# Attention scores issued as pinned pairs of matmuls, and the order of ScalarE's and VectorE's last instructions

## The chip, the cores and the metric

One Trainium2 chip, one of its cores. The metric is the device time of one execution in microseconds. The engines are called by the profile's names: PE is TensorE (matmuls), PEld its weight loads, DVE is VectorE, ACT is ScalarE, POOL is GpSimd, SP is SyncE, which here only starts DMAs.

## What is computed

A trunk of two layers over 256 tokens of width 1024, in float32. Each layer is: half a SwiGLU feed-forward (hidden width 2816), three attentions side by side with a gate each, another half feed-forward, and a gated addition of a second input `p`. At the end there is one more RMS norm.

```
for i in range(2):
    h = h + 0.5 * swiglu(rms_norm(h, g0), ffn1_wi, ffn1_wo)
    n = rms_norm(h, g1); split n @ w_in into the q, k, v, gates of A, B and C
    ya = differential attention (4 heads x 2 score maps, all earlier keys)
    yb = NSA attention (8 heads: compressed keys, selected blocks, window)
    yc = sliding window attention with sinks (8 heads, window 128)
    h = h + (sig(ga) * (ya @ wb0) + sig(gb) * (yb @ wb1) + sig(gc) * (yc @ wb2)) @ w_out
    h = h + 0.5 * swiglu(rms_norm(h, g2), ffn2_wi, ffn2_wo)
    h = h + sig(rms_norm(h, g3) @ w_ple_gate) * (p[i] @ w_ple)
return rms_norm(h, final_norm)
```

All score heads have width 64: `s = q k^T / 8 + bias`, then a masked softmax.

## The kernel before

**Products.** The tokens are two tiles `t` of 128. Every float32 operand `x` is split into a rounded part `hi` and a rest `lo`, both of a reduced type, and a product is three matmuls, `hi hi + hi lo + lo hi` (`mul3`, lines 265 to 268). Weights come in pieces of 128 x 1024 by a DMA on SyncE's queue (line 375). ScalarE makes `hi` of a piece and VectorE `lo` (`split`, lines 256 to 263). `product` (line 402) runs over the contraction's blocks `k` for both token tiles, the second some steps behind the first, and accumulates in one PSUM bank of 512 columns per tile. When a tile is done, a function `done` reads the bank with ScalarE and VectorE.

**Attentions beside the products.** Three generators, `attend_a`, `attend_c` and `attend_b`, each handle units of four score rows: `first` makes the scores and the softmax of a unit, `second` turns the probabilities and multiplies them with the values of the unit before. After each step of a product `flow.tick()` lets the running generator go on by a piece, so that attention work and products alternate in the program's text. `flow.join` finishes a generator where its result is needed. Each layer calls `scores` fourteen times: four units of A, four of C, six of B.

**scores (line 958).** A call takes two PSUM banks, `ps[0]` and `ps[1]`, from the tag `s`, which has two buffers in all, so the next call needs the same two banks again. For two blocks of heads `m`, for the three products `(x, y)` of hi and lo, and for `par` 0 and 1, it issues one matmul: the contraction is 64 rows deep, and `par` chooses the upper or lower 64 rows of the array. Half `par` writes to `ps[par]`. So twelve matmuls are written per call, with the two halves alternating in the text. They have 128 columns where only one key tile is visible (token tile 0 of A and C), and 256 elsewhere. `softmax` (line 972) reads the four rows one after the other on VectorE (line 978), `ps[0]` first, then `ps[1]`, and ScalarE takes the exponential (line 980).

**What sets the order.** The kernel is written as one program, and a planner decides the order on each engine before it runs. The planner simulates the engines with estimates of its own. Whenever an engine is free, it gives it, among the instructions whose inputs and buffers are ready, the one with the lowest turn; the turn is the place in the text. Two things change that. `tc.high_priority(offset=n)` moves what is written inside it n turns ahead. `tc.keep_in_program_order(ins)` puts `ins` behind the instruction written just before it on the same engine; it orders the issue and waits for no completion, and others may still come in between. On the chip each engine then runs its instructions in the planned order and waits on semaphores. In the kernel before, the score matmuls have neither: each of the twelve takes its own turn.

**The last product.** In the second layer the gate product of the last addition (`ple`, line 1519) runs its second half of columns with `last_product` (line 390): first token tile 0 with 512 columns, then token tile 1 in two quarters of 256, here called third and last quarter. Each ends in `gate.done` (line 1534): tanh on ScalarE (line 1537), the gate product with `pp` on VectorE (line 1538), then `residual_last.done` (line 509): the residual added into `h` on VectorE (line 512), the sum of squares on ScalarE (line 514), for the third quarter also the product of `h` with the final norm's weight into `hg` (`finish`, line 537) and two small sums of statistics (lines 517, 518). The last quarter closes the statistics (line 521), GpSimd takes the power -1/2 (line 522), and `finished` (line 539) scales the rows and sends them out on the queues of ScalarE and SyncE.

Of the kernel before, what the change touches and what calls it, by code (L numbers as in the profile page):

```python
# [13 lines left out]
AF = mybir.ActivationFunctionType  # L14
ALU = mybir.AluOpType
AX = mybir.AxisListType

D, SEQ, DEPTH = 1024, 256, 2
PLE, DFF = 256, 2816
EPS = 1e-6  # L20
# [197 lines left out]
def trunk(ctx: ExitStack, tc: tile.TileContext, a: dict, out: bass.AP, index: list):  # L218
    nc = tc.nc
# [30 lines left out]
    def stage(name="stage"):  # L250
        return base.tile([128, 512], F32, tag="stage", bufs=4, name=name)
# [169 lines left out]
    class Norm:  # L421
# [44 lines left out]
        def square(self, t, c):  # L466
            sq = stage("sq")
            nc.scalar.activation(sq, h[:, t, 512 * c:512 * c + 512], AF.Square, accum_out=self.stat[t][:, c:c + 1])

        def finish(self, t):  # L470
            st = self.stat[t]
            nc.vector.tensor_scalar(st[:, 2:3], st[:, 0:1], 1.0 / D, EPS, op0=ALU.mult, op1=ALU.add)
            nc.vector.scalar_tensor_tensor(st[:, 2:3], st[:, 1:2], 1.0 / D, st[:, 2:3], op0=ALU.mult, op1=ALU.add)
            nc.gpsimd.tensor_tensor(st[:, 3:4], st[:, 2:3], mhalf[:, 0:1], op=ALU.pow)
            nc.vector.tensor_scalar(st[:, 4:5], st[:, 3:4], 0.5, None, op0=ALU.mult)
            nc.vector.tensor_scalar(st[:, 5:6], st[:, 3:4], 0.125, None, op0=ALU.mult)
# [13 lines left out]
    def residual(norm, c, scale, final=False):  # L490

        s = slice(512 * c, 512 * c + 512)

        def done(t, ps):
            nc.vector.scalar_tensor_tensor(h[:, t, s], ps, scale(t), h[:, t, s], op0=ALU.mult, op1=ALU.add)
            if final:
                finish(t, 0, 512)
            elif c == 0 and norm.row % 2:
                norm.turn_late(t)
            else:  # L500
                norm.turn(t, c)
            norm.square(t, c)
            if c == 1:
                norm.finish(t)
        return done

    def residual_last(norm, scale):

        def done(t, x, s):
            o = slice(512 + s.start, 512 + s.stop)  # L510
            st = norm.stat[t]
            nc.vector.scalar_tensor_tensor(h[:, t, o], x, scale(t), h[:, t, o], op0=ALU.mult, op1=ALU.add)
            sq = stage("sq")[:, :s.stop - s.start]
            nc.scalar.activation(sq, h[:, t, o], AF.Square, accum_out=st[:, 6:7] if s.start else st[:, 1:2])
            if s.stop < 512:
                finish(t, 512, 768)
                nc.vector.tensor_scalar(st[:, 2:3], st[:, 0:1], 1.0 / D, EPS, op0=ALU.mult, op1=ALU.add)
                nc.vector.scalar_tensor_tensor(st[:, 2:3], st[:, 1:2], 1.0 / D, st[:, 2:3], op0=ALU.mult, op1=ALU.add)
                return
            if s.start:  # L520
                nc.vector.scalar_tensor_tensor(st[:, 2:3], st[:, 6:7], 1.0 / D, st[:, 2:3], op0=ALU.mult, op1=ALU.add)
                nc.gpsimd.tensor_tensor(st[:, 3:4], st[:, 2:3], mhalf[:, 0:1], op=ALU.pow)
            else:
                norm.finish(t)
            finished(t, s.start, norm.r(t))
        return done

    last = []

    def finish(t, start, stop):  # L530

        if not last:
            last.append(base.tile([128, SUB], F32, tag="raw", bufs=RAWS, name="gfin"))
            nc.sync.dma_start(last[0], rows(a["gfin"], [[1, D]]))
            last.append(base.tile([128, NT, D], F32, tag="blk", bufs=6, name="hg"))
        gfin, hg = last
        nc.vector.tensor_tensor(hg[:, t, start:stop], h[:, t, start:stop], gfin[:, start:stop], op=ALU.mult)

    def finished(t, extra, r):

        gfin, hg = last
        y = [stage("out") for _ in range(2)]
        nc.scalar.activation(y[0], hg[:, t, :512], AF.Copy, scale=r)
        o = slice(512 + extra, 1024)
        nc.vector.scalar_tensor_tensor(y[1][:, extra:], h[:, t, o], r, gfin[:, o], op0=ALU.mult, op1=ALU.mult)
        if extra:
            nc.vector.tensor_scalar(y[1][:, :extra], hg[:, t, 512:512 + extra], r, None, op0=ALU.mult)
        for k, queue in enumerate((nc.scalar, nc.sync)):
            queue.dma_start(out[t * 128:(t + 1) * 128, 512 * k:512 * k + 512], y[k])
# [366 lines left out]
    def attention(i, norm, after):  # L916
# [41 lines left out]
        def scores(name, q, qb, t, key):  # L958

            ps = [psum.tile([128, 2, 256], F32, tag="s", bufs=2, name=name) for _ in range(2)]  # L960
            for m in range(2):
                for x, y in ((0, 0), (0, 1), (1, 0)):
                    for par in range(2):
                        r = slice(64 * par, 64 * par + 64)
                        kk = key(y, r, m)
                        o = ps[par][:, m, :math.prod(kk.shape[1:])]
                        if len(kk.shape) == 3:
                            o = o.rearrange("p (s n) -> p s n", s=kk.shape[1])
                        nc.tensor.matmul(o, q[r, x, qb[m], t * 128:(t + 1) * 128], kk, start=x + y == 0, stop=x == 1)  # L969
            return ps  # L970

        def softmax(p, ps, bias, sink=None):
# [57 lines left out]
        def attend_a():  # L1030
            bnd = band(0)

            def first(u):
                m, t = u
                nk = 128 * (t + 1)
                s = scores("s", qk[m], [0, 1], t, lambda x, r, k: qk[m][r, x, 2 + k, :nk])
                yield
                p = pool.tile([128, 4, 256], F32, tag="p", bufs=3, name="p")
                st = None
                for st in softmax([p[:, j, :nk] for j in range(4)], [s[j // 2][:, j % 2, :nk] for j in range(4)],  # L1040
                                  [back(bnd[:, 2 * m + j % 2], nk) for j in range(4)]):
                    yield
                nc.vector.reciprocal(st[:, 8:12], st[:, 4:8])
                nc.vector.tensor_scalar(st[:, 10:12], st[:, 10:12], nlam[:, i:i + 1], None, op0=ALU.mult)
                for x in range(2):
                    nc.vector.tensor_scalar(p[:, 2 + x, :nk], p[:, 2 + x, :nk], st[:, 10 + x:11 + x], None, op0=ALU.mult)
                    nc.vector.scalar_tensor_tensor(p[:, x, :nk], p[:, x, :nk], st[:, 8 + x:9 + x], p[:, 2 + x, :nk],
                                                   op0=ALU.mult, op1=ALU.add)
                yield
                return p  # L1050
# [221 lines left out]
        def attend_b():  # L1272
            bnd, y_ps = {}, {}

            def first(u):
# [3 lines left out]
                if t == 0:  # L1279
                    p = pool.tile([128, 4, 2, 128], F32, tag="p", bufs=3, name="p")  # L1280
                    s = scores("s", qB[0], [2 * g, 2 * g + 1], 0, lambda x, r, m: kB[0][r, x, g:g + 3:2, :128])
                    rows = [(j, k) for j in range(4) for k in range(2)]
                    pr = [p[:, j, k] for j, k in rows]
                    sr = [s[j // 2].rearrange("p m (k n) -> p m k n", k=2)[:, j % 2, k] for j, k in rows]
                    br = [back(bnd[g][:, j], 128) for j, k in rows]
                else:
                    p = pool.tile([128, 4, 256], F32, tag="p", bufs=3, name="p")
                    s = scores("s", qB[0], [2 * g, 2 * g + 1], 1, lambda x, r, m: kB[0][r, x, 2 * ss[0] + g, :])
                    pr = [p[:, j] for j in range(4)]
                    sr = [s[j // 2][:, j % 2] for j in range(4)]  # L1290
                    br = [back(bnd[g][:, j], 256) for j in range(4)]
# [265 lines left out]
    h = base.tile([128, NT, D], F32, name="h")  # L1557
# [17 lines left out]
    def rows(src, steps):  # L1575
        return bass.AP(tensor=src.tensor, offset=src.offset, ap=[[0, 128]] + steps)
# [141 lines left out]
```

## Time and profile before

| | us |
|---|---|
| median of 3 runs | 1306.7 |
| lowest and highest | 1305.04, 1307.22 |
| the profiled execution | 1305.41 |
| its span | 1303.6 |
| mean granted clock of TensorE in it | 0.998 |

The span reaches from the first to the last instruction of the profiled execution. In a row of the page's groups or of the timeline stand the line of the kernel, the engine, the operation, the tiles written and read, and the shapes (`64*128 64x256` is a stationary operand of 64 rows and 128 columns and a moving one of 64 rows and 256 columns). Starts are microseconds from the beginning of the span. Matmuls overlap in their pipeline, so the time one of them costs is the distance to the start of the next, not its own duration; the chain of waits counts in that way. In the chain in order of time, a row is start, time added to the chain, engine, tile written, line, and xN for N equal instructions in a row.

### The profile page before, as it was taken

The page shows a single profiled execution, that of the slowest core. Times are in us where ns is not written, and L with a number is a line of the kernel's source. Part 1 is how long each engine was busy: PE and PEld are TensorE (multiplying, and loading weights), DVE is VectorE, ACT ScalarE, POOL GpSimd, SP SyncE. Part 2 cuts the span into 40 slices and gives each one's busy share as a digit, 9 for nine tenths or more (in the row PEclk, how much of TensorE's full clock was granted, in tenths as well). Part 3 has the DMA queues.
Part 4 walks back from the last instruction along what each step waited for, and adds up shares of the span by engine and source line. Part 5 has one row for each costly group of instructions (what it writes and reads, how often), then busy time and mean ns, then how long its engine had stood idle before and what let it go on. Part 6 is the DMA issues. An engine that isn't in the chain of part 4 may idle for free.

```text
span 1303.6 us, 17964 instructions
## 1 busy us (share of the span) xinstructions
PE 1293.1 (99%) x6250; PEld 1067.2 (82%) x6250; DVE 1092.4 (84%) x1754; ACT 923.6 (71%) x1468; POOL 28.7 (2%) x46
## 2 busy tenths in 40 slices
PE   9999999999999999999999999999999999999997
PEld 7888888887888888888888888888888888888886
DVE  7878977768978799997799999677687888999975
ACT  7677667658858577876667876666696775877664
POOL 0000000000000000000000000000000000000000
PEclk9999999999999999999999999999999999999999
DMA  8778787455743567687666787865556435677772
GB/s 318 227 230 267 203 262 221 125 181 173 227 151 108 181 191 239 213 239 213 210 196 228 208 248 234 249 175 163 176 173 199 162 129 182 205 211 230 230 231 85
DMA packets 137180, 263.76 MB, mean 202 GB/s; under 512 B 71670, under 2 KB 77174, under 8 KB 137088
## 3 DMA queue, kind: packets, MB, share of 16 engines
q1 hardware_dynamic: 134128, 252.57, 62.7%
q0 software_dynamic: 2528, 9.47, 2.2%
q8 instruction: 49, 0.80, 0.3%
q10 hardware_dynamic: 432, 0.56, 0.1%
q14 instruction: 43, 0.35, 0.1%
HBM read 245.75 MB, written 1.08 MB: 189 GB/s over the span
## 4 chain that ended last, share of the span: by engine, by line
PE 98%; DMA 0%; issue 0%; ACT 0%; SPq 0%; DVE 0%; POOLq 0%; POOL 0%; DVEq 0%; ACTq 0%
PE ff L267 8%; PE ff L266 8%; PE ff L268 8%; PE fo L267 5%; PE fo L266 5%; PE fo L268 5%; PE p L266 4%; PE p L268 4%; PE p L267 4%; PE gate L266 4%; PE gate L268 3%; PE gate L267 3%; PE s L969 3%; PE A L267 2%; PE br L266 2%; PE A L266 2%
## 5 line engine op out<-in xcount | busy, mean ns | idle before, releaser
L254 DVE TENSOR_TENSOR wl<-raw,wh 128x1024 fp32r<-128x1024 f32 (+1 forms) x426 | 510.1, 1211 | 96.2 <-ACT wh L259 94.5
L259 ACT ACTIVATE wh<-raw 128x1024 fp32r<-128x1024 f32 (+1 forms) x426 | 441.7, 1047 | 152.1 <-DMA raw<-in_wst 66.1
L267 PE MATMUL ff<-wl,nT 128*128 128x512 f32 x464 | 180.9, 390 | 0.0
L268 PE MATMUL ff<-wh,nT 128*128 128x512 f32 x464 | 180.3, 390 | 0.0
L266 PE MATMUL ff<-wh,nT 128*128 128x512 f32 x464 | 171.7, 390 | 0.0
L268 PE MATMUL fo<-wh,gT 128*128 128x512 f32 x304 | 117.1, 389 | 0.0
L267 PE MATMUL fo<-wl,gT 128*128 128x512 f32 x304 | 115.7, 389 | 0.0
L266 PE MATMUL fo<-wh,gT 128*128 128x512 f32 x304 | 114.2, 390 | 0.0
L267 PEld LDWEIGHTS ff<-wl,nT 128*128 128x128 f32 x464 | 87.1, 188 | 18.2 <-DVE wl L254 0.2
L268 PEld LDWEIGHTS ff<-wh,nT 128*128 128x128 f32 x464 | 87.1, 188 | 18.0
L266 PEld LDWEIGHTS ff<-wh,nT 128*128 128x128 f32 x464 | 87.1, 188 | 18.0
L268 PE MATMUL gate<-wh,nT 128*128 128x512 f32 x192 | 76.6, 399 | 0.0
L266 PE MATMUL gate<-wh,nT 128*128 128x512 f32 x192 | 76.4, 399 | 0.0
L267 PE MATMUL gate<-wl,nT 128*128 128x512 f32 x192 | 75.8, 395 | 0.0
L268 PEld LDWEIGHTS fo<-wh,gT 128*128 128x128 f32 x304 | 57.1, 188 | 11.8
L266 PEld LDWEIGHTS fo<-wh,gT 128*128 128x128 f32 x304 | 57.1, 188 | 11.7
L267 PEld LDWEIGHTS fo<-wl,gT 128*128 128x128 f32 x304 | 57.1, 188 | 11.7
L980 ACT ACTIVATE p<-p,st 128x128 f32<-128x128 f32 (+1 forms) x128 | 56.7, 449 | 5.3 <-DVE st L978 5.0
L568 ACT ACTIVATE whole<-flip 128x1024 uint16<-128x1024 uint16 x32 | 43.0, 1365 | 20.4 <-DMA flip<-cut 20.3
L562 ACT ACTIVATE cut<-gated 128x1024 uint16<-128x1024 uint16 (+1 forms) x48 | 46.3, 974 | 9.9 <-DVE gated L608 9.9
L254 DVE TENSOR_TENSOR wl<-x,wh 128x1024 fp32r<-128x1024 f32 x42 | 50.5, 1219 | 2.5 <-ACT wh L259 2.5
L259 ACT ACTIVATE wh<-x 128x1024 fp32r<-128x1024 f32 x42 | 43.7, 1048 | 7.0 <-DVE x L254 5.8
(395 smaller groups left out, 2780.5 us busy)
## 6 DMA issues: line engine op xcount, KB each, us to landing
raw<-in_wst SPq DMA_DIRECT2D x424, 512.0 KB, 4.4
y<-in_wst POOLq DMA_DIRECT2D x6, 1024.0 KB, 6.8
band<-table SPq DMA_DIRECT2D x10, 512.0 KB, 5.2
xy<-in_wst POOLq DMA_DIRECT2D x4, 512.0 KB, 4.1
raw<-in_wbv SPq DMA_DIRECT2D x4, 420.0 KB, 3.2
xt<-in_xt SPq DMA_DIRECT2D x4, 256.0 KB, 5.5
raw<-in_wst SPq DMA_DIRECT2D x4, 256.0 KB, 5.0
h<-in_x SPq DMA_DIRECT2D x2, 512.0 KB, 8.0
```

The lines of the kernel that those rows point to most:

```text
L254: nc.vector.tensor_tensor(o, x, y, op=ALU.subtract)
L259: nc.scalar.activation(hi, src, AF.Copy)
L266: nc.tensor.matmul(ps, xh, wh, start=start, stop=False, **kw)
L267: nc.tensor.matmul(ps, xh, wl, start=False, stop=False, **kw)
L268: nc.tensor.matmul(ps, xl, wh, start=False, stop=stop, **kw)
L562: nc.scalar.activation(cut.rearrange("p (w n) -> p w n", w=2), halves(src)[:, :128 * m].rearrange("p n w -> p w n"), AF.Copy)
L568: tc.keep_in_program_order(nc.vector.tensor_copy(to, of) if late else nc.scalar.activation(to, of, AF.Copy))
L969: nc.tensor.matmul(o, q[r, x, qb[m], t * 128:(t + 1) * 128], kk, start=x + y == 0, stop=x == 1)
L980: nc.scalar.activation(p[j], p[j], AF.Exp, bias=st[:, j:j + 1], scale=-1.0, accum_out=st[:, n + j:n + j + 1])
```

## The change

`scores` puts its matmuls two to twelve 300 turns ahead and behind one another; the first keeps its own turn and is tied to nothing. In the tail, the third quarter's square, `hg` product and small sums are written into a function `rest`, which is kept in `put_off` and called only when the last quarter's tanh, gate product and residual have been written. That residual and the `hg` product are tied to their place in the order of VectorE. The last quarter's square carries the factor 1/D itself (a scale of D to the power -1/2 before squaring), so that the last small operation is a plain sum.

```
+            add = nc.vector.scalar_tensor_tensor(h[:, t, o], x, scale(t), h[:, t, o], op0=ALU.mult, op1=ALU.add)
+            if put_off:
+                tc.keep_in_program_order(add)
+                put_off.pop()()
             sq = stage("sq")[:, :s.stop - s.start]
-            nc.scalar.activation(sq, h[:, t, o], AF.Square, accum_out=st[:, 6:7] if s.start else st[:, 1:2])
+
+            def square():
+                nc.scalar.activation(sq, h[:, t, o], AF.Square, scale=D ** -0.5 if s.start else 1.0,
+                                     accum_out=st[:, 6:7] if s.start else st[:, 1:2])
+
             if s.stop < 512:
-                finish(t, 512, 768)
-                nc.vector.tensor_scalar(st[:, 2:3], st[:, 0:1], 1.0 / D, EPS, op0=ALU.mult, op1=ALU.add)
-                nc.vector.scalar_tensor_tensor(st[:, 2:3], st[:, 1:2], 1.0 / D, st[:, 2:3], op0=ALU.mult, op1=ALU.add)
+                def rest():
+                    square()
+                    finish(t, 512, 768)
+                    nc.vector.tensor_scalar(st[:, 2:3], st[:, 0:1], 1.0 / D, EPS, op0=ALU.mult, op1=ALU.add)
+                    nc.vector.scalar_tensor_tensor(st[:, 2:3], st[:, 1:2], 1.0 / D, st[:, 2:3], op0=ALU.mult, op1=ALU.add)
+                put_off.append(rest)
                 return
+            square()
             if s.start:
-                nc.vector.scalar_tensor_tensor(st[:, 2:3], st[:, 6:7], 1.0 / D, st[:, 2:3], op0=ALU.mult, op1=ALU.add)
+                nc.vector.tensor_tensor(st[:, 2:3], st[:, 6:7], st[:, 2:3], op=ALU.add)
                 nc.gpsimd.tensor_tensor(st[:, 3:4], st[:, 2:3], mhalf[:, 0:1], op=ALU.pow)
...
-    last = []
+    last, put_off = [], []
...
-        nc.vector.tensor_tensor(hg[:, t, start:stop], h[:, t, start:stop], gfin[:, start:stop], op=ALU.mult)
+        x = nc.vector.tensor_tensor(hg[:, t, start:stop], h[:, t, start:stop], gfin[:, start:stop], op=ALU.mult)
+        if start:
+            tc.keep_in_program_order(x)
...
-                        nc.tensor.matmul(o, q[r, x, qb[m], t * 128:(t + 1) * 128], kk, start=x + y == 0, stop=x == 1)
+                        with tc.high_priority(offset=0 if (m, x, y, par) == (0, 0, 0, 0) else 300):
+                            ins = nc.tensor.matmul(o, q[r, x, qb[m], t * 128:(t + 1) * 128], kk, start=x + y == 0, stop=x == 1)
+                        if (m, x, y, par) != (0, 0, 0, 0):
+                            tc.keep_in_program_order(ins)
```

More of the change, by code (lines that the diff above doesn't have):

```diff
@@ L511, in done @@
             st = norm.stat[t]
-            nc.vector.scalar_tensor_tensor(h[:, t, o], x, scale(t), h[:, t, o], op0=ALU.mult, op1=ALU.add)
+            add = nc.vector.scalar_tensor_tensor(h[:, t, o], x, scale(t), h[:, t, o], op0=ALU.mult, op1=ALU.add)
+            if put_off:
+                tc.keep_in_program_order(add)
+                put_off.pop()()
             sq = stage("sq")[:, :s.stop - s.start]
-            nc.scalar.activation(sq, h[:, t, o], AF.Square, accum_out=st[:, 6:7] if s.start else st[:, 1:2])
+            def square():
+                nc.scalar.activation(sq, h[:, t, o], AF.Square, scale=D ** -0.5 if s.start else 1.0,
+                                     accum_out=st[:, 6:7] if s.start else st[:, 1:2])
             if s.stop < 512:
-                finish(t, 512, 768)
-                nc.vector.tensor_scalar(st[:, 2:3], st[:, 0:1], 1.0 / D, EPS, op0=ALU.mult, op1=ALU.add)
-                nc.vector.scalar_tensor_tensor(st[:, 2:3], st[:, 1:2], 1.0 / D, st[:, 2:3], op0=ALU.mult, op1=ALU.add)
+                def rest():
[4 more added lines that the diff above has]
+                put_off.append(rest)
                 return
+            square()
             if s.start:
-                nc.vector.scalar_tensor_tensor(st[:, 2:3], st[:, 6:7], 1.0 / D, st[:, 2:3], op0=ALU.mult, op1=ALU.add)
+                nc.vector.tensor_tensor(st[:, 2:3], st[:, 6:7], st[:, 2:3], op=ALU.add)
                 nc.gpsimd.tensor_tensor(st[:, 3:4], st[:, 2:3], mhalf[:, 0:1], op=ALU.pow)
```

## The prediction

> **What bounds the kernel now.** I read the page first, for the engine that sets the end.
>
> ```profile
> span 1303.6 us, 17964 instructions
> PE 1293.1 (99%) x6250; PEld 1067.2 (82%) x6250; DVE 1092.4 (84%) x1754; ACT 923.6 (71%) x1468; POOL 28.7 (2%) x46
> ...
> PE 98%; DMA 0%; issue 0%; ACT 0%; SPq 0%; DVE 0%; POOLq 0%; POOL 0%; DVEq 0%; ACTq 0%
> ```
>
> TensorE is busy for 99% of the span, and the chain that ended last is 98% TensorE. So a nanosecond taken out of TensorE's stream is a nanosecond off the span, as long as no other engine becomes late by it. A busy TensorE can still waste time in how its matmuls follow each other, so the second view is the chain in order of time. There each row is a run of equal instructions with what it added to the chain. These are the score runs (L969) of the first layer, without three more undivided calls of 0.91, 0.91 and 0.92 us.
>
> ```profile
> 211.20 0.37 PE s L969 x3
> 211.56 0.43 PE A L267
> 211.99 0.23 PE A L268
> ...
> 213.15 0.26 PE s L969 x2
> ...
> 214.76 0.26 PE s L969 x2
> ...
> 220.69 0.26 PE s L969 x2
> ...
> 221.85 0.36 PE s L969 x3
> ...
> 226.23 0.91 PE s L969 x12
> 227.14 0.32 PE Ck L268
> 227.46 0.12 PE Ck L266
> ...
> 233.12 0.59 PE s L969 x7
> ...
> 234.09 0.48 PE s L969 x5
> ...
> 261.78 0.82 PE s L969 x12
> ...
> 297.98 1.10 PE s L969 x12
> ...
> 303.33 0.54 PE s L969 x3
> ...
> 304.31 0.55 PE s L969 x3
> ...
> 305.52 0.55 PE s L969 x3
> ...
> 306.49 0.55 PE s L969 x3
> ...
> 316.61 0.31 PE s L969
> ...
> 321.41 0.78 PE s L969 x9
> ...
> 325.42 0.31 PE s L969 x2
> ...
> 330.67 0.91 PE s L969 x6
> ...
> 331.84 0.90 PE s L969 x6
> ...
> 336.68 1.25 PE s L969 x12
> ...
> 386.99 0.55 PE s L969 x6
> ...
> 387.98 0.55 PE s L969 x6
> ...
> 401.36 0.67 PE s L969 x7
> ...
> 404.29 0.54 PE s L969 x5
> ```
>
> A call of `scores` issues twelve matmuls of 64 rows each: for each of two heads `m`, three products, each on both halves `par` of the array's rows. Three things are to be seen. **Order inside a run:** at 226.23 twelve matmuls of 256 columns take 0.91 us; at 330.67 six of the same size take 0.91 us too. Twelve at the price of six is what comes out when neighbours sit on different row halves and run together; the six at 330.67, then six more for 0.90, are one half after the other and run singly. At 336.68 the order is mixed (1.25). **Undivided and paired** a call costs 0.91 us at 256 columns, and 0.82 at 128 columns (261.78). **Each run has a border price:** the first full-height matmul behind a run takes 0.32 instead of 0.12 (227.14 against 227.46), or 0.43 instead of 0.23 (211.56 against 211.99), so 0.20 us for every run, however short.
>
> **The score part, step by step.** Nine of a layer's fourteen calls are divided or out of order. By their rows they cost 0.37+0.26+0.26+0.26+0.36 = 1.51 (five runs), 0.59+0.48 = 1.07 (two), 1.10 (one), 0.54+3x0.55 = 2.19 (four), 0.31+0.78+0.31 = 1.40 (three), 0.91+0.90 = 1.81 (two), 1.25 (one), 0.55+0.55 = 1.10 (two), 0.67+0.54 = 1.21 (two): 12.64 us. Undivided and paired, the first three (128 columns: first token tile of the A and C attentions) would cost 3x0.82 and the other six 6x0.91, 7.92 together: 4.72 less. They make 22 runs where 9 would do: 13 borders of 0.20, 2.60. So at most 7.32 us per layer; the second layer has the same code and the same shapes, so 14.6 for both. The other five calls are already undivided and paired; I cost the edit at nothing there.
>
> What the change does to the order: matmuls two to twelve each stand behind the one before in TensorE's order, and 300 places ahead of their turn. So nothing with a later turn, and little with an earlier one, gets in between once each is ready. That repairs divisions that came from other work having its turn (211.20, 233.12, 316.61, 386.99, 401.36) and the order inside the run. It can't repair a second PSUM bank that is not free yet: the two halves write two banks, and the bank of half 1 comes free later, because the softmax reads half 0 first. The calls at 303.33 and 330.67 finish half 0 before half 1 begins, which is how the plan would look if bank 1 were late. With the pin the first matmul goes alone and eleven follow when bank 1 is free. A single one costs 0.31 (316.61) plus a border of 0.20, about 0.5. The trace has no pinned call, so its price is bounded from both sides: nothing, or 0.5 for each of a layer's fourteen calls, 7.0, which leaves 0.3 of the 7.32. I take 0.5 for the two calls just named and half of it for the two whose order is mixed (297.98 and 336.68): 1.5. That is 7.32 - 1.5 = 5.8 per layer, **11.6 us** for both layers.
>
> Nothing else is issued: the same 336 matmuls, no DMA, nothing on the queues of SyncE or GpSimd. Work that is passed over is moved by less than 1 us at a time; it sits on TensorE too, and its readers are covered as long as the other engines keep their slack (third rival).
>
> **The tail, step by step.** The timeline of the last microseconds:
>
> ```profile
> 1294.85 0.28 PE L268 MATMUL pg<-wh,nT 128*128 128x256 f32 x1
> ...
> 1295.51 0.42 ACT L514 ACTIVATE sq<-h 128x256 f32<-128x256 f32 x1 [0.95 <-DVE h L512]
> ...
> 1295.92 0.46 ACT L1537 ACTIVATE th<-pg,stats 128x256 f32<-128x256 f32 x1
> 1297.39 0.42 ACT L514 ACTIVATE sq<-h 128x256 f32<-128x256 f32 x1 [1.01 <-DVE h L512]
> ```
>
> The last matmul ends at 1294.85 + 0.28 = 1295.13, but the last quarter's tanh begins at 1295.92, behind the third quarter's square, for which ScalarE sat idle. Put ahead of it, the tanh begins up to 0.79 us earlier, and gate product, residual and square follow it. The third quarter's square (1295.92 - 1295.51 = 0.41) then falls into the 1.01 us in which ScalarE waits for the last residual, so it is covered; without that cover it would cost its 0.41. On VectorE the `hg` product and two small sums now come behind the last residual, beside the last square. The product is of the same size as the square (0.42), the sums are small; I put 0.1 for them being late for the statistics. Folding 1/D into the square only replaces one small operation by another. Bounds: -0.1 to +0.8; I take **0.7**, since in the trace the tanh's input is complete before the square's (0.95 us of waiting ended at 1295.51 only), so nothing has to hold the tanh back.
>
> **Sum.** 11.6 + 0.7 = 12.3 us. The profiled execution took 1305.41 us, its span being 1303.6; that gives 1293.1. The shown runs have a median of 1306.7 (1305.04 to 1307.22), 1.3 above it, which gives 1294.4. I forecast **1294**. By the bounds of the two parts the gain is 0.3x2 - 0.1 = 0.5 to 14.6 + 0.8 = 15.4.
>
> **Rivals.**
>
> (1) *The plan breaks most calls into one and eleven*, since bank 1 is late nearly always: the change then does not do what it says. Gain 0.6 + 0.7 = 1.3, so 1305.4. For it: the calls at 303.33 and 330.67. Against: calls such as 226.23 and 261.78 alternate halves from their first matmul without a pin, so both banks were free.
>
> (2) *Slower: TensorE stops in order.* The planner works from its own estimate of VectorE. If a pinned run is issued before the softmax has really left bank 1, TensorE stands still, since it can't pass the waiting matmul; behind it stand all products, and VectorE, ScalarE and the weight buffers wait for those. The price is the reading of half 1's two heads:
>
> ```profile
> L978 DVE CUSTOM_DVE_ANT_0 p<-s,band x96: 280/354/425, 222.4 to 1049.1; 128x128 f32<-128x128 f32 x48, 128x256 f32<-128x256 f32 x48
> ...
>   PEld s L969: 0.7, 2
> ```
>
> Two median reduces are 2 x 0.354 = 0.71 us. It decides from 12.3 / 0.71 = 18 of the 28 calls; in all of them it is 19.9, a loss of 7.6 and 1314.3. Against it: over the whole kernel the score matmuls waited for this reduce twice, 0.7 us in all, as the second row counts.
>
> (3) *Half is given back.* TensorE arrives sooner at the merge of the third attention, and the chain of softmax, turning and gathering is not shortened. The stretches of the attention's second half:
>
> ```profile
> 320.00:380.00 60.00, 60.00 (x338) 50.54 (x337) 50.19 (x117) 40.97 (x88) 0.00 (x0) 1.00 0.64 209
> 380.00:425.00 45.00, 45.00 (x241) 36.33 (x240) 40.54 (x100) 37.66 (x83) 0.00 (x0) 1.00 0.36 116
> ```
>
> The columns are stretch, its length, then busy time of TensorE, weight loads, VectorE and ScalarE. VectorE has 40.54 of 45 us. What I expect to save in a layer's six calls from 316 on is 0.89 + 0.60 + 0.09 + 0.39 + 0.50 = 2.5 (the fifth is already whole). If that comes back as waiting at the merge, 5.0 of the 12.3 are gone: gain 7.3, 1299.4. Against: the saving inside this last stretch is 0.9, and 40.54 of 44.1 is 92%, still short of full. The Trainium skill ("TensorEngine Tiling (Array Packing)", Performance Considerations, PSUM Bottleneck) warns in this sense: packing row tiles makes TensorE faster but not the emptying of PSUM, which may then be the limit. By that rule the time would be that of this rival; the rows so far speak for it only in the last stretch.
>
> **How the numbers follow.** Forecast 0.64 (1289.5 to 1297.5); half given back 0.15; one and eleven 0.11; slower 0.10. The first two hold 0.79, so the range goes from 1289.5 (a gain of 15.4, counted from the lower of the shown runs) to 1300.5. A measurement here can tell about 0.2%, 2.6 us, from no change. Faster: 0.64 + 0.15 + a third of the one-and-eleven case, 0.82; the rest of that case, 0.08, is no change; slower 0.10. The forecast's own gain reaches from 9 to 15.4.
>
> **What would show it.** In the chain after, L969 should fall from 34 us (two layers of 12.64 and the five whole calls' 4.47) to about 25-27, in 28 to 36 rows instead of 54, nearly all of them x12 (0.91, or 0.82 at 128 columns) or x1 followed by x11; rows with x6 of 0.9 should be gone. Rows `x1` in most calls mean rival 1. Idle time of TensorE before L969 released by `st` L978 of several us means rival 2; idle time before `br` or `wo`, released by VectorE's `yB` or `mT`, means rival 3. In the tail, the last tanh should begin within 0.1 us of the last matmul's end, with the third quarter's square behind it; if the square is still ahead, the 0.7 is wrong. A fall of the score rows with an unchanged time would make the whole reading wrong, that TensorE's stream is the time.

## The result and the profile after

| | kernel before | kernel after |
|---|---|---|
| median, us | 1306.59 (4 runs) | 1298.62 (4 runs) |
| lowest and highest | 1305.04, 1307.22 | 1298.43, 1299.48 |
| profiled execution | 1305.41 | 1298.72 |
| its span | 1303.6 | 1296.9 |
| clock of TensorE | 0.998 | 0.998 |

The ratio is 0.9942, with a 95% interval from 0.9925 to 0.9959: 8.0 us by the medians, 6.7 us by the two profiled executions. Timed a second time (below, with another set of the kernel before) the changed kernel had the same median, 1298.62, against 1305.32: 6.7 us. So the gain is 6.7 to 8.0 us where 12.3 were forecast.

The page of the changed kernel: span, busy time of the engines, and the chain that ended last by engine.

```profile
span 1296.9 us, 17954 instructions
PE 1284.1 (99%) x6250; PEld 1062.0 (82%) x6250; DVE 1091.2 (84%) x1754; ACT 922.5 (71%) x1468; POOL 27.6 (2%) x46
...
PE 92%; ACT 3%; DVE 2%; issue 1%; DMA 1%; SPq 0%; POOLq 0%; POOL 0%; DVEq 0%; ACTq 0%
```

TensorE is still busy for 99%, but its share of the chain has gone from 98% to 92%. What is new there is ScalarE 3% and VectorE 2%: at some places TensorE now waits for them. These shares are not waiting time: where TensorE waited, the chain goes back along the engine that it waited for, often for many instructions. The busy row hides this, since 1% of 1297 us is 13 us.

**The score runs.** The chain of the changed kernel in order of time; the columns are start, time added, engine, tile and line (the scores are now line 983), number of instructions. The chain leaves out matmuls that run beside their pair, so a run of eleven can show as x9 or x10.

```profile
226.50 0.82 PE s L983 x12
...
290.74 0.31 PE s L983
291.05 0.43 PE br L266
291.47 0.23 PE br L267
291.71 0.91 PE s L983 x9
...
296.39 0.81 PE s L983 x11
```

No call is in more than two runs, and every twelve or eleven but one has the paired price: 0.90 to 0.91 us, 0.81 to 0.82 at 128 columns. The one, at 968 us, took 1.29 because its second matmul came 0.42 us behind its first. But nine of the 28 calls begin with a single matmul, six in the first layer and three in the second. The one at 290.74 shows the price: 0.31 for itself and 0.43 instead of 0.23 for the first `br` product behind it. Counted by the distances between the starts of TensorE's matmuls, the runs fell from 54 to 37 and their sum from 34.2 to 27.7 us: 6.5, and 17 borders of 0.20, together 9.9 us.

**The waits.** In the stretch in which the compression runs (`cmp`, in each layer 64 matmuls that use up eight pieces of `w1`) beside the end of a gate product, both kernels are shown by their waits (engine and line, what it waited for; us, times, longest), first the changed kernel, then the kernel before:

```profile
PEld gate L267 <- DVE wl L254: 1.3, 1, 1.3
PE gate L267 <- DVE wl L254: 1.0, 1, 1.0
PEld gate L266 <- ACT wh L259: 1.0, 1, 1.0
PE gate L266 <- ACT wh L259: 0.7, 1, 0.7
```

```profile
ACT wh L259 <- PE br L268: 1.4, 1, 1.4
ACT wh L259 <- DMA raw<-in_wst: 0.9, 1, 0.9
...
```

Before, no wait of TensorE for a weight piece stands in the list, and ScalarE waited for TensorE to free a weight buffer; the pieces were ahead. After, TensorE waits for the rounded part `wh` of a piece from ScalarE and for the rest `wl` from VectorE. The windows of these stretches (start and end, length, then busy us with instruction counts of TensorE, weight loads, VectorE, ScalarE, GpSimd, then clock, DMA share, GB/s), changed kernel first:

```profile
318.00:336.00 18.00, 16.25 (x121) 13.80 (x120) 17.44 (x50) 17.88 (x57) 0.00 (x0) 1.00 0.51 163
...
953.00:975.00 22.00, 21.11 (x148) 17.37 (x147) 21.83 (x64) 21.34 (x59) 0.00 (x0) 1.00 0.59 192
```

```profile
318.00:338.00 20.00, 20.00 (x139) 16.98 (x138) 19.47 (x56) 17.34 (x45) 0.00 (x0) 1.00 0.67 223
```

VectorE is busy for 97% here after (17.44 of 18) and was for 97% before (19.47 of 20); ScalarE went from 87% to 99%. So VectorE had no slack in this stretch before the change either. In the second layer's copy of it VectorE has 21.83 of 22 us after. Which work filled them is in the groups of 318 to 336 us, changed kernel first, then the kernel before (line, engine, operation, tiles, shapes, count, busy us and mean ns, idle time before):

```profile
L254 DVE TENSOR_TENSOR wl<-raw,wh 128x1024 fp32r<-128x1024 f32 x7 | 8.4, 1218 | 0.1
L259 ACT ACTIVATE wh<-raw 128x1024 fp32r<-128x1024 f32 x6 | 6.3, 1050 | 0.0
L996 ACT ACTIVATE p<-p,st 128x128 f32<-128x128 f32 x16 | 6.2, 390 | 0.0
...
L1322 DVE TENSOR_SCALAR p<-p,st 128x128 f32<-128x128 f32 x8 | 1.8, 278 | 0.0
```

```profile
L254 DVE TENSOR_TENSOR wl<-raw,wh 128x1024 fp32r<-128x1024 f32 x8 | 9.6, 1216 | 0.8 <-ACT wh L259 0.8
L259 ACT ACTIVATE wh<-raw 128x1024 fp32r<-128x1024 f32 x8 | 8.4, 1052 | 2.2 <-PE br L268 1.4 <-DMA raw<-in_wst 0.9
...
L980 ACT ACTIVATE p<-p,st 128x128 f32<-128x128 f32 x9 | 3.5, 388 | 0.0
```

In the same 18 us ScalarE now makes six pieces instead of eight and VectorE seven instead of eight; sixteen exponentials stand where nine stood, and B's scaling (line 1322, line 1306 before) is there eight times, where its first one came at 339.8 before. In this layer B's first softmax was pulled ahead of weight pieces. Whether that is why the pieces are late is asked below; the second layer differs.

**The account.** By TensorE's starts, in us:

| | score runs and borders | waits | sum | measured |
|---|---|---|---|---|
| first attention part (first `A` product to last `wo`) | -4.4 | 0.86 + 1.21 | -2.3 | -2.07 |
| second attention part | -5.5 | 0.46 + 0.66 + 0.28 + 0.63 | -3.5 | -3.39 |
| tail, last matmul's end to the end of the span | | | | -0.69 |
| all else | | | | -0.5 |

The measured column sums to the span's 6.7. The waits are those at the compression, in both layers, but for the 0.63 at 1055 (`mt`, the transposes at the merge, for `pT` from VectorE). About 4.1 of the 9.9 us came back as waiting, 3.5 of them for weight pieces. The 0.46 does not come every time: it follows a wait of ScalarE for a DMA (`w2raw`, at 941 us) of 1.28 us here, and in the changed kernel's second profile (`e9_changed_again`), with 0.57 us for that DMA, it is absent.

**The tail** of the changed kernel, from the timeline (start, duration, engine, line, operation):

```profile
1288.84 0.28 PE L268 MATMUL pg<-wh,nT 128*128 128x256 f32 x1
...
1289.16 0.47 ACT L1553 ACTIVATE th<-pg,stats 128x256 f32<-128x256 f32 x1 [0.61 <-PE pg L268]
1289.53 0.41 ACT L519 ACTIVATE sq<-h 128x256 f32<-128x256 f32 x1
...
1290.65 0.42 ACT L519 ACTIVATE sq<-h 128x256 f32<-128x256 f32 x1 [0.61 <-DVE h L512]
```

The tanh begins at 1289.16, 0.04 after the last matmul's end (1288.84 + 0.28 = 1289.12), and the third quarter's square lies in ScalarE's wait for the last residual.

### The profile page after: what moved, and what is told of

Its sections match the earlier page's. It is cut to its first block, busy times and chain, and to the rows that moved or that the text cites. A ratio compares the mean times of both kernels' runs of the same rounds, so it can differ in the third digit from the quotient of the medians.

```text
span 1296.9 us, 17954 instructions
## 1 busy us (share of the span) xinstructions
PE 1284.1 (99%) x6250; PEld 1062.0 (82%) x6250; DVE 1091.2 (84%) x1754; ACT 922.5 (71%) x1468; POOL 27.6 (2%) x46
## 4 chain that ended last, share of the span: by engine, by line
PE 92%; ACT 3%; DVE 2%; issue 1%; DMA 1%; SPq 0%; POOLq 0%; POOL 0%; DVEq 0%; ACTq 0%
PE ff L267 8%; PE ff L266 8%; PE ff L268 8%; PE fo L268 5%; PE fo L266 5%; PE fo L267 5%; PE p L266 4%; PE p L267 4%; PE p L268 4%; PE gate L266 3%; PE gate L267 3%; PE gate L268 3%; PE A L267 2%; PE A L268 2%; PE A L266 2%; PE s L983 1%
```

## The experiments

The diffs are against the changed kernel. Each time is compared with the kernel before, timed beside it on the same chip; the chips of different experiments differ. "Score sum" and "runs" are counted as above (before: 34.2 us in 54 runs; after: 27.7 in 37). Two accounts of the lost 4 us stand against each other in the expectations. The theory, T: in the stretch of the compression VectorE and ScalarE are full, so TensorE runs into late weight pieces there, whoever saved its time ahead of it. The rival, R: it is the order; the pins let B's scores, and so B's softmax, come early, and it stands ahead of the weight pieces.

### Scores alone, tail alone

`e1_scores_only` has the new score loop and the old tail, `e2_tail_only` the reverse:

```
-                        with tc.high_priority(offset=0 if (m, x, y, par) == (0, 0, 0, 0) else 300):
-                            ins = nc.tensor.matmul(o, q[r, x, qb[m], t * 128:(t + 1) * 128], kk, start=x + y == 0, stop=x == 1)
-                        if (m, x, y, par) != (0, 0, 0, 0):
-                            tc.keep_in_program_order(ins)
+                        nc.tensor.matmul(o, q[r, x, qb[m], t * 128:(t + 1) * 128], kk, start=x + y == 0, stop=x == 1)
```

> Only the pins and the priority of the score matmuls; the tail is that of the kernel before. Theory T (late weights): the score part takes 9.9 us out of TensorE's stream (6.5 in the score runs, 17 borders fewer at 0.20) and loses about 4.4 us as TensorE waits for weight pieces near 320-336 and 955-975 us, where ScalarE and VectorE are both over 95% busy. Then this kernel is about 7.3 us below the kernel before (1299.3), with the same waits in the same places, and 0.7 us above the changed kernel. Rival (the waits come with the tail's changed plan): near 1296, without the waits.

> Only the tail's new order; the score matmuls as before. Every theory expects the score runs of the kernel before (54 runs, 34 us) and a stretch from the end of the last matmul to the end of the span of 7.8 us instead of 8.5: 0.7 us below the kernel before, 1305.9. If the tail has changed more than that (a part of the 8 us that the whole change gains), it is seen here.

Measured against 1305.44: scores alone 1299.74 (1299.34 to 1300.62), ratio 0.9957 (0.9942 to 0.9972), with the same 37 runs (27.3 us) and the same waits at the compression, 0.86 and 1.21 in the first layer. Tail alone 1304.71 (1303.98 to 1306.42), ratio 0.9996 (0.9987 to 1.0006), with 54 runs and 34.2 us as before. Its tail takes 7.78 us instead of 8.51; a gain of 0.7 is too small to show in the time. The two parts add up: 5.7 + 0.7 = 6.4.

### The pins on two attentions, and on the third

`e3_only_a_and_c` pins and puts ahead only the calls of A and C, `e10_only_b` only those of B (`is` instead of `is not`):

```
+            pinned = q is not qB[0]
-                        with tc.high_priority(offset=0 if (m, x, y, par) == (0, 0, 0, 0) else 300):
+                        with tc.high_priority(offset=300 if pinned and (m, x, y, par) != (0, 0, 0, 0) else 0):
-                        if (m, x, y, par) != (0, 0, 0, 0):
+                        if pinned and (m, x, y, par) != (0, 0, 0, 0):
```

> Pins and priority for the calls of attentions A and C only; B's calls each at their own turn; tail as changed. By their rows A and C save 6.8 us of TensorE time in both layers, the tail 0.7. Theory T (the stretch before and in the compression is at the limit of ScalarE and VectorE, whoever saves TensorE time ahead of it): about 4 us of it come back as waits, 1303. Rival R (the waits exist because B's scores now go ahead, so their softmax stands before the splitting of weights): no waits over those of the kernel before, 1299.

> Pins and priority for B's six calls only; A and C at their own turn; tail as changed. Theory R (B's scores ahead put B's first softmaxes in front of the splitting of weights, and TensorE waits for these as much as B's runs save): beside the tail's 0.7 nothing, within 1 us of it: 1304 to 1305.5, with waits for weights in the compression. Rival T (the lost time is a matter of how much TensorE time is saved ahead of the compression, whoever saves it): B alone saves little ahead of it, so no waits come, and it gains its 4 us and the tail's 0.7: 1300.5.

A and C alone: 1299.69 (1298.95 to 1300.85), ratio 0.9957 (0.9943 to 0.9971). The runs are 42 and their sum 30.7 us, so TensorE saved 3.5 + 12 x 0.20 = 5.9, and the two attention parts are 5.1 us shorter: nearly all of it is kept. At the compression TensorE does not wait in either layer; it waits once later, at 347 us, for the gate's tanh (the kernel's waits):

```profile
PEld br L266 <- ACT th L1418: 1.3, 1, 1.3
```

By T, time saved ahead of the compression should have met late pieces too. In the first layer it did not, though TensorE began the compression at 322.0 us, earlier than the changed kernel (323.1), and VectorE had 19.76 of the 20 us from 318 to 338. With the same tail, scores alone would stand at 1299.74 - 0.7 = 1299.0; so pinning B as well brings 0.7 us, out of 3.0 + 5 x 0.20 = 4.0 that it takes off the score runs. For the first layer this speaks for R and against T as it was put. But even there R fits only in part. The groups of the A-and-C kernel from 318 to 336 us are nearer to the changed kernel's than to those of before:

```profile
L259 ACT ACTIVATE wh<-raw 128x1024 fp32r<-128x1024 f32 x7 | 7.4, 1051 | 1.2 <-PE br L268 1.2
L997 ACT ACTIVATE p<-p,st 128x128 f32<-128x128 f32 x16 | 6.2, 389 | 0.0
```

Sixteen exponentials stand here too, with seven splits on each engine. B's first scores start at 313.0 us (312.9 in the changed kernel), only its second call comes later (325.0 against 318.4).

For the second layer the traces decide against R. ScalarE runs the same instructions in the same order in both kernels, from the layer's first `A` product to 973 us. These are VectorE's splits near the end of the compression there, by the timeline (start, duration, engine, line, operation), in the changed kernel and then in the A-and-C kernel:

```profile
970.81 2.35 DVE L254 TENSOR_TENSOR wl<-raw,wh 128x1024 fp32r<-128x1024 f32 x2
973.08 0.87 DVE L1322 TENSOR_SCALAR p<-p,st 128x128 f32<-128x128 f32 x4
```

```profile
970.54 1.21 DVE L254 TENSOR_TENSOR wl<-raw,wh 128x1024 fp32r<-128x1024 f32 x1
971.67 0.87 DVE L1323 TENSOR_SCALAR p<-p,st 128x128 f32<-128x128 f32 x4
972.46 2.35 DVE L254 TENSOR_TENSOR wl<-raw,wh 128x1024 fp32r<-128x1024 f32 x2
```

The changed kernel has two pieces in front of B's scaling and TensorE waits; the A-and-C kernel has one of them behind it and TensorE does not. What differs is TensorE. In `e9_changed_again` the first of these pieces is done at 971.82 us, in the A-and-C kernel at 971.75; TensorE's last product in front of the wait starts at 970.97 in the one and at 972.11 in the other. It is 1.1 us earlier where B's calls are whole, and it waits 0.67 and 0.27. So here the saved time runs into VectorE's splits, as T has it.

B alone: 1313.85 (1313.4 to 1314.07) against 1305.32, ratio 1.0064 (1.0051 to 1.0076): 8.5 us slower than before, which no theory had expected. Its chain at A's calls, which it does not pin:

```profile
226.35 1.02 PE s L984 x12
233.36 0.81 PE s L984 x7
234.54 0.70 PE s L984 x5
246.14 0.31 PE s L984
246.87 0.79 PE s L984 x9
248.25 0.31 PE s L984 x2
```

The calls of 226, 233 and 246 us cost 0.91, 0.59 + 0.47 and 0.91 before; here 1.02, 0.81 + 0.70 and 1.41 in three runs. In all there are 67 runs and 37.1 us: 2.9 + 13 x 0.20 = 5.5 us more than before. TensorE's starts show 3.9 us of waits besides (1.2 and 2.7 in the two layers), none of them for a weight piece; so R's waits at the compression did not come either. The parts of this edit do not add (each with the new tail): -5.7 for A and C, +8.5 for B, -6.7 for both. One difference from the kernel before is not isolated: an unpinned call stands here in a priority block of offset 0, before in none. So why A's and C's calls fall apart when only B's are pinned stays open.

### The priority without the pins

```
-                        if (m, x, y, par) != (0, 0, 0, 0):
-                            tc.keep_in_program_order(ins)
```

> The eleven matmuls have their 300 turns of priority but no tie to one another; tail as changed. If the single first matmul in front of eleven comes from the second bank, it should be gone here, with the price that one half goes through before the other: runs of 12 at 1.2 to 1.8 us instead of 0.91 in those calls. If the pins cost nothing and the order within a run stays paired, TensorE saves 6.5 + 24 borders x 0.20 = 11.3 us. First theory: between 1299 and 1302; second: 1296.

1298.34 (1297.95 to 1299.86), ratio 0.9948 (0.9933 to 0.9963): what the changed kernel has. The calls are contiguous without a pin, 30 runs, but some go one half after the other, at the price of unpaired ones (chain of this kernel):

```profile
295.22 0.81 PE s L983 x6
...
296.30 0.81 PE s L983 x6
```

So the priority alone makes the runs whole, and the pins only keep the halves alternating: 28.4 us in 30 runs against 27.7 in 37. That is 0.7 us more in the runs and 1.4 less at their borders, and TensorE waits as much (in the first layer 1.29 at 334.5 us and 1.40 at 348.7, the second of them for the gate's tanh). The time is 0.7 us below the range that the first theory had given (1299 to 1302).

### Why nine calls begin with a single matmul

`e5_both_banks` lets the first matmul of a call wait for the last softmax reduce of the call before, so that both PSUM banks are free when the group starts:

```
+        read = []
...
+                        if read and (m, x, y, par) == (0, 0, 0, 0):
+                            tc.add_manual_dep(ins.ins, read[0].ins.name, mybir.DependencyInfo(mybir.DependencyClass.Sync, mybir.DependencyReason.DATA), reason="bank")
...
+                read[:] = [nc.vector.tensor_tensor_reduce(out=p[j], in0=ps[j], in1=bias[j], scale=-1.0, scalar=low,
+                                               op0=ALU.add, op1=ALU.min, accum_out=st[:, j:j + 1])]
```

> As the changed kernel, and the first matmul of a call also waits for the last softmax read of the call before, that is until both PSUM banks are free. If the single first matmuls of the changed kernel come from the second bank, there are 28 runs of 12 and none of 1 and 11: nine singles at 0.31 + 0.20 fewer, 4.5 us of TensorE time. The part of it ahead of the compression (two us in four calls) should be lost again to the weight pieces that are late there, the other 2.5 us stay: 2.5 us below the changed kernel, about 1296. Rival (the singles have another cause): the runs 1 and 11 stay and the time is that of the changed kernel.

1296.22 (1295.95 to 1296.44) against 1305.37, ratio 0.9929 (0.9916 to 0.9941). All 28 calls are now one run (chain of this kernel):

```profile
292.07 0.90 PE s L985 x12
...
299.54 0.82 PE s L985 x12
```

The sum is 24.95 us in 28 runs: 9.25 + 26 x 0.20 = 14.45 us less than before, the prediction's upper end of 14.6. The singles were waits for the second bank. The time is 2.4 us below the changed kernel's 1298.62 for a 4.5 us better score sum with borders. TensorE's waits have grown from 4.1 to 5.0 us, and they have moved. These rows are from the compression and from the merge of the first layer:

```profile
PEld cmp L1181 <- DVE wl L254: 1.1, 2, 0.8
...
PE cmp L1181 <- DVE wl L254: 0.4, 1, 0.4
...
PE mt L274 <- DVE pT L254: 0.5, 1, 0.5
```

By the starts, 3.1 us of both layers lie at the compression (3.5 in the changed kernel) and 1.9 at the merge (0.63 there), where the transposes wait for B's turned probabilities. B's first scaling stands at 332.1 us here, as late as in the A-and-C kernel (332.7) and 9 us later than in the changed kernel, and still TensorE waits for `wl`. So B's early softmax is not needed for these waits.

### B's first calls in their own turn

With both banks awaited, the first three B calls of a layer are neither pinned nor put ahead:

```
-        def scores(name, q, qb, t, key):
+        def scores(name, q, qb, t, key, pinned=True):
...
-                    s = scores("s", qB[0], [2 * g, 2 * g + 1], 0, lambda x, r, m: kB[0][r, x, g:g + 3:2, :128])
+                    s = scores("s", qB[0], [2 * g, 2 * g + 1], 0, lambda x, r, m: kB[0][r, x, g:g + 3:2, :128], False)
...
+                    s = scores("s", qB[0], [2 * g, 2 * g + 1], 1, lambda x, r, m: kB[0][r, x, 2 * ss[0] + g, :], g + ss[0] > 0)
```

> As e5, but the first three of B's six calls keep their own turn, without pins and priority. Theory R (the waits for weight pieces come from B's first softmaxes being pulled in front of the splitting of weights): the waits near 320-336 and 955-975 us are gone, as with A and C alone, and the late calls' saving stays: 12 to 13 us below the kernel before. Rival T (any TensorE time saved ahead of the compression is lost there): the waits are as in the changed kernel, 8 to 10 us below the kernel before.

1296.32 (1296.01 to 1296.65), ratio 0.993 (0.9918 to 0.9943), 30 runs, 25.7 us, and the waits of `e5_both_banks`. The edit hardly moved the plan: B's first scaling is at 332.3 us here and at 332.1 there. So the comparison of the two says nothing on T and R; the order that R blames was not changed.

### Half of the compression's weight pieces

`e7_before_half_the_w1_pieces` and `e8_after_half_the_w1_pieces` take the kernel before and after and use every second piece of `w1` twice, so that half of the loads and splits of the compression are left out and TensorE's work stays (the compressed keys and values are therefore other ones):

```
-                    wh, wl = w1(16 * kv + k)
+                    wh, wl = w1(16 * kv + k // 8 * 8 + k % 4)
...
-        w1 = streamed(i, "w1", 256)
+        w1 = streamed(i, "w1", 256, False)
+        for j in range(0, 8, 2):
+            w1.push(j)
```

> The kernel before, with every second weight piece of the compression left out and its neighbour used twice (the compressed keys and values are therefore other ones): the same matmuls, but per layer four pieces fewer to load and to split (4.2 us of ScalarE, 4.9 of VectorE). TensorE waits for no weights in the kernel before, so every theory expects its time within 1 us of the kernel before.

> The changed kernel with the same pieces left out as in e7. Theory (about 4 us of the score part's saving are lost because ScalarE and VectorE are late with weight pieces at the compression): the waits go away, and the distance to e7 is that of the TensorE time saved, 10 to 11 us, instead of 8. Rival (the score part saves only 8 us and the waits replace waits of the kernel before elsewhere): the distance stays at 8.

The kernel before with half the pieces took 1310.43 (1309.81 to 1310.62) against 1305.37, ratio 1.0037 (1.0023 to 1.005). That missed its expectation: less work, and slower, because the plan came out otherwise: 60 score runs of 37.2 us. So it is no clean baseline. The changed kernel with half the pieces took 1294.54 (1294.4 to 1295.33), ratio 0.9917 (0.9904 to 0.9931), with the changed kernel's score runs (38, 27.6 us). Its window at the compression of the first layer:

```profile
320.00:333.00 13.00, 13.00 (x101) 11.92 (x100) 12.39 (x43) 12.94 (x41) 0.00 (x0) 1.00 0.39 126
```

TensorE is busy all the time, with no wait of more than 0.23 us in either attention part, and the time is 4.1 us below the changed kernel's 1298.62. That is the size of the waits in the account above. Against the kernel before it is 10.8 us, about all that the score runs and the tail save (6.6 + 16 x 0.20 + 0.7 = 10.5). So fewer pieces end the waits; they cost about 4 us, though the plan is not quite the same (B's third call stands at 334.1 us instead of 327.8). B's first scaling is as early as in the changed kernel (323.6 us against 323.3), so its early softmax alone does not make TensorE wait. VectorE and ScalarE are as full as in the changed kernel (12.39 and 12.94 of 13), so a full engine alone does not either; what counts is whether the pieces are among what it has done by then.

### Taking work off ScalarE and off VectorE

Both start from `e5_both_banks`. `e11_both_banks_c_scaling_on_gpsimd` moves the 16 scalings per layer of C's softmax from ScalarE to GpSimd, `e12_both_banks_b_scaling_on_gpsimd` those of B's first token tile that VectorE makes (8 per layer):

```
-                    nc.scalar.activation(pr[j], pr[j], AF.Copy, scale=st[:, 12 + j:13 + j])
+                    nc.gpsimd.tensor_scalar(pr[j], pr[j], st[:, 12 + j:13 + j], None, op0=ALU.mult)
```
```
-                        nc.vector.tensor_scalar(pr[j], pr[j], of, None, op0=ALU.mult)
+                        (nc.gpsimd if t == 0 else nc.vector).tensor_scalar(pr[j], pr[j], of, None, op0=ALU.mult)
```

> As e5, and the sixteen scalings of probabilities per layer in attention C (four per unit, 0.32 us each) go from ScalarE to GpSimd, which is idle. If ScalarE's load near 300-335 us is what makes the weight pieces late, 5 us per layer less of it there should remove most of the 1.9 us of waits per layer that e5 shows in the compression: 2 to 4 us below e5. If GpSimd's scalings are slow, or take memory time from VectorE, the C attention ends later and the gain is gone: at e5 or above it.

> As e5, and the eight scalings per layer that VectorE makes for B's first two units (0.28 us alone, 0.22 in a row) go to GpSimd. e11 took 5 us per layer from ScalarE near the compression and the waits for weight pieces stayed. If VectorE's load is what makes the pieces late there, about 1.8 us per layer less of it should take 1 to 2 us per layer off TensorE's waits in the compression: 2 to 4 us below e5 and e11. Rival (what is late is the chain of softmax, turning and splitting, not a full engine; GpSimd's 0.9 us per scaling makes that chain longer): at e5 or above, with the waits as there.

C's scalings on GpSimd: 1295.57 (1295.31 to 1295.93) against 1305.32, ratio 0.9923 (0.991 to 0.9937). ScalarE was relieved by 4.9 us between 290 and 333 us (34.65 busy instead of 39.59), but TensorE's waits for `wl` stay (windows and waits of this kernel):

```profile
290.00:320.00 30.00, 30.00 (x179) 24.09 (x178) 26.40 (x63) 22.34 (x53) 13.77 (x15) 1.00 0.57 179
320.00:333.00 13.00, 11.83 (x99) 10.05 (x96) 12.50 (x47) 12.31 (x38) 1.34 (x2) 1.00 0.61 192
```

```profile
PE gate L267 <- DVE wl L254: 0.6, 1, 0.6
```

So taking C's share off ScalarE does not end the waits; VectorE still has 12.50 of 13. The time is 0.65 us below `e5_both_banks` (another chip), where 2 to 4 were expected, and the two profiled spans are the same. B's scalings on GpSimd: 1297.66 (1296.54 to 1298.51) against 1305.47, ratio 0.9942 (0.9928 to 0.9956), 1.4 us above `e5_both_banks` where 2 to 4 below were expected. TensorE's waits for `wl` fall, from 1.1 and 0.4 us to the second row here, and another takes their place:

```profile
PE pt L274 <- POOL p L1326: 1.7, 1, 1.7
...
PEld cmp L1181 <- DVE wl L254: 0.3, 1, 0.3
```

The scaling lies on B's own chain, and GpSimd is slower at it, so the transposes of B's probabilities wait. Whether the pieces are in time because VectorE has less to do, or because TensorE, held for 1.7 us at the transposes, comes to them later, this run can't say.

### The changed kernel again

> The changed kernel once more, beside e10 and e11 on the same chip. 8 us below the kernel before, as measured first; 2.4 us above e5 if that difference is more than one of chips.

1298.62 (1297.95 to 1299.42) against 1305.32, ratio 0.9948 (0.9935 to 0.996), with 37 runs of 27.3 us and the waits of 0.86 and 1.21 at the compression of the first layer; its waits sum to 3.6 us. Its range does not touch that of `e5_both_banks` (1295.95 to 1296.44, on another chip whose kernel before took 1305.37), nor that of the version with C's scalings on GpSimd, on the same chip: both are below the two kernels, the latter by 9.75 us against the kernel before.

## Why the prediction was right in direction and short in size

The time, 1298.62, lies in the range (1289.5 to 1300.5), above the forecast 1294, outside the forecast's own 1289.5 to 1297.5, and next to the third rival's 1299.4. So the account that was given 0.64 missed the size, and the range held only because it took in a rival that was given 0.15.

- **Prices: right.** Paired and whole at 0.91 and 0.82, 0.31 for a single, 0.20 per border: all as read in the trace of before. `e5_both_banks` reached 14.45 of the 14.6 worked out as the most that can be saved.
- **How many singles: too few.** The prediction took 1.5 us per layer (two calls, and half the price for two), 3.0 in all. There were nine of about 0.5, six in the first layer and three in the second, 4.5 us. It looked for late second banks only in calls that went half after half or in mixed order; in fact calls that were paired in the old order (387 us) got a late bank too, presumably since contiguous scores bring TensorE there earlier. And it took the second layer to have the first one's plan. The score part saved 9.9 instead of 11.6.
- **The step that failed** is "a nanosecond taken out of TensorE's stream is a nanosecond off the span, as long as no other engine becomes late by it", together with "its readers are covered as long as the other engines keep their slack". The slack was looked for from 320 to 380 us and from 380 on, where VectorE has 84% and 90%. These means hide the first 18 us, in which VectorE had 97% before already. And it was looked for in the readers of the scores; what came late was the weight pieces, which share both engines with the readers. Of the 9.9 us 4.1 came back, 3.5 for pieces and 0.6 at the merge.
- **Rival 3** had the size (5.0 of 12.3 given back) and the mechanism, TensorE early for the other engines, but not the place: the waits stand before `gate` and `cmp`, released by `wl` and `wh`, not before `br` and `wo`, released by `yB` and `mT`. Only the 0.63 at 1055 us lies at the merge, for `pT`. Its 5.0 us were worked out as the whole saving of B's calls, so that they come near the 4.1 is in part luck. The late emptying of the score banks shows in the singles, not in these waits. With both banks awaited the merge gives back more, 1.9 us.
- **Rival 1** (one and eleven) came in 9 of 28 calls, not in most. **Rival 2** (stop in order for the second bank) fits at most one call: the run of twelve at 968 us took 1.29 instead of 0.91, and in the second profile of the same kernel it took 0.91.
- **The tail: right.** 0.69 of 0.7, the tanh 0.04 behind the last matmul, the square under the residual.
- **Signs named beforehand:** 27.7 us and 37 rows, where 25 to 27 and 28 to 36 were named: just missed, by the singles. No unpaired sixes: right.

**What is settled and what is not.** The waits for weight pieces go when half of the pieces are left out, and about 4 us with them: shown. The singles are second-bank waits: shown by `e5_both_banks`. Taking C's scalings off ScalarE doesn't end the waits: shown. In the second layer the pieces are not late because of B's softmax, since VectorE is done with them no later than in the A-and-C kernel; TensorE is earlier, and VectorE, busy for 21.83 of 22 us, has no room to be: shown by the rows. In the first layer B's second call and its softmax come earlier with the pins, and fewer pieces are done by then; that these pieces are late for this reason is argued from the groups and the A-and-C run, and `e5_both_banks` shows waits without it. The one run that was to put B's order back by itself did not move it. What share the order has in the first layer, and what share the load, stays open.

## What to carry to other kernels

Look for the slack of the other engines in stretches of 10 to 20 us around each saving, and over all that runs on them, weight preparation too: an engine with 84% on the mean can be full just where TensorE arrives earlier. A group of matmuls that only pays as a whole should start when all its buffers are free, not when its first one is; here that alone was worth 2.4 us. And with a planner between the text and the chip, do not add up parts: the same pins, each time with the new tail, were worth -5.7 on two attentions, +8.5 on the third and -6.7 on all.

## What was not expected of the hardware

GpSimd needs far longer for a scaling of one operand by one value per row than the other engines, as a view of that line in three kernels shows (ns: least, median, most; the first GpSimd with C's, the second VectorE with B's, the third ScalarE with C's; 16 of 128 and 16 of 256 columns each):

```profile
L1394 POOL TENSOR_SCALAR p<-p,st x32: 597/925/1715, 289.8 to 958.8; 128x128 f32<-128x128 f32 x16, 128x256 f32<-128x256 f32 x16
```

```profile
L1322 DVE TENSOR_SCALAR p<-p,st x32: 272/316/356, 323.3 to 1044.3; 128x128 f32<-128x128 f32 x16, 128x256 f32<-128x256 f32 x16
...
L1390 ACT ACTIVATE p<-p,st x32: 385/448/510, 291.3 to 958.9; 128x128 f32<-128x128 f32 x16, 128x256 f32<-128x256 f32 x16
```

A median of 925 ns against 316 and 448, and up to 1715. GpSimd had little else to do (2% busy in the kernel before), and still its scaling brought at most 0.65 us with C, and cost 1.4 with B, where TensorE waited for it.
